# Decay blocks' subtractions issued behind later VectorE work, and the mixer's output product with its first low-input matmuls put last

## Chip, core and metric

The kernel runs on one core of one Trainium2 chip, as one launch. The metric is the device time in microseconds; for the kernel before it is 1547.75 us, the median of three runs (1547.63 to 1549.64).

## What is computed

Two layers (`DEPTH = 2`) of a decoder on a sequence of 256 tokens with 1024 channels, all in fp32. A layer is a half-step SwiGLU FFN, a token mixer, and a second FFN. The mixer normalises its input, multiplies it by one wide matrix and runs two branches on the result: a Mamba-2 branch (SSD, in two chunks of 128 tokens) and a gated DeltaNet branch (four chunks of 64). Both branches' outputs go through a matrix, are gated, added, and multiplied by `w_out`. What matters here, cut from the reference:

```
seg = a_cum[:, :, :, None] - a_cum[:, :, None, :]
decay = jnp.where(causal, jnp.exp(jnp.where(causal, seg, 0.0)), 0.0)
cb = jnp.einsum("bclgn,bcsgn->bclsg", Cc, Bc)
y_diag = jnp.einsum("bclsg,bclsgh,bcsghp->bclghp", cb, decay, xdt)
...
merged = (jax.nn.sigmoid(gate_s) * (y_s @ ssm_w_branch[l])
          + jax.nn.sigmoid(gate_d) * (y_d @ dn_w_branch[l]))
h = h + merged @ w_out[l]
```

The decay is needed for 32 heads; they come in four groups of eight, and a "decay block" is one group's `exp(seg)` for both chunks, masked and multiplied by `cb`: 128 x 2048 numbers.

## The kernel before, in words

**Products.** Every weight tile (128 x 1024) comes in by DMA as `wraw` and is split into two rounded parts: ScalarE (ACT) copies it to `whi` (L67), VectorE (DVE) subtracts to get `wlo` (L70, `prep`, L173 to L194). Inputs are split in the same way into a high and a low part. A product is then three matmuls on TensorE (PE): high x high, high x low, low x high (`mm3`, L315, and `mm3w`, L320). There are five buffers each of `whi` and `wlo` (`NSPL = 5`), taken in turn, so a new `whi` waits until PE has done with the tile five before it.

**The mixer's order.** The mixer is a list of steps written out by hand (`ORDER`, L45 to L49), run by `step` (L1170). Around the change it reads, in the program's order: `P` (`ssd_pre`, L999: for each group the product `cbb` of B and C on PE, masked on DVE into `cbt`), the gate units `g100 g101`, `D0` (`decay(0)`), `S0` (first half of `ssd(0)`, L1048), `x10` (convolved inputs of group 1), `T0` (second half of `ssd(0)`), `D1`, `x11`, gates, `S1`, `x20`, `T1`, `o` (`dn_T(0)`), `x21`, `N` (the DeltaNet branch's matrix, `dn_branch`), `D2`, `y` (`ss_T(0)`), `S2`, `D3` and so on. The scheduler places each engine's instructions in its own queue out of this order; a queue runs in order, and an instruction that waits holds up all that stand behind it.

**decay(g)** (L1020 to L1035): a DMA on SP's queue brings 1 MB of broadcast rows into `dc` (two buffers, `sA` and `sB`, so block 2 takes block 0's); DVE subtracts `ac` (L70, `dc<-dc,ac`); DVE takes the minimum with 0 (L77); ACT takes the exponential (L67, `dc<-dc`); DVE multiplies by `cbt` (L70, `dc<-dc,cbt`). PE reads `dc` in `ssd`'s products `ydb` (L1076).

**ssd(g)**: PE turns the convolved inputs `xsT` (made by ACT behind three DVE steps `ca`) into `xsb` (L1062); DVE scales them to `xD`, `xdt` and `xe`; then `ydb` and `yob` on PE, sums into `yz` on DVE, their squares `jk` on ACT, the sum's `sss` on DVE (L78), a power -0.5 `srr` on GpSimd (POOL, L209), and two scalings of `yz` by it on ACT.

**The DeltaNet branch's matrix**: `dn_T(hp)` (L1111) turns `vb` on PE into `oT` (L1115), DVE gates it to `og`, ACT rounds that to the high part `bh`, DVE subtracts to the low part `bl`. PE multiplies them in `b` (L316 to L318).

**The output product** is `close` (L399), which calls `out_chunks` (L366): for the two row halves t = 0, 1 it takes every weight tile k and column half n. Its input is made by `merge(t)` (L1217): `mT` on PE (L1225), `mh` on ACT, `ml` on DVE. The FFNs' output products go through `close_blocks` and call `out_chunks` without the new argument.

Of the kernel before, what the change touches and what calls it, by code (L numbers as in the profile page):

```python
# [11 lines left out]
ALU = mybir.AluOpType  # L12
# [4 lines left out]
P = 128  # L17
# [7 lines left out]
GS = 4  # L25
# [27 lines left out]
def trunk_kernel(ctx, tc, x, wst, wsm, norms, lpar, rpar, cst, out):  # L53
    nc = tc.nc
    V, A, G, PE = nc.vector, nc.scalar, nc.gpsimd, nc.tensor
# [10 lines left out]
    def act(o, i, func=AF.Copy, **kw):  # L66
        return A.activation(out=o, in_=i, func=func, **kw)  # L67

    def tt(o, a, b, op):
        return V.tensor_tensor(out=o, in0=a, in1=b, op=op)  # L70
# [4 lines left out]
    def ts(o, a, s1, op0, sc2=None, op1=None):  # L75
        if op1 is None:
            return V.tensor_scalar(out=o, in0=a, scalar1=s1, scalar2=None, op0=op0)  # L77
        return V.tensor_scalar(out=o, in0=a, scalar1=s1, scalar2=sc2, op0=op0, op1=op1)  # L78
# [7 lines left out]
    def trb(name):  # L86
        return trp.tile([P, 512], F32, tag="tr", name=name)
# [4 lines left out]
    def small(shape, name, bufs=2):  # L92
        return sm.tile(shape, F32, tag=name, name=name, bufs=bufs)
# [54 lines left out]
    state = {"loaded": 0, "prepped": 0, "taken": 0, "last": None, "hold": False, "behind": {}, "late": {}, "first": 0}  # L148
# [52 lines left out]
    def take():  # L201
        j = state["taken"]
        state["taken"] = j + 1
        ahead("loaded", limit[min(j + NSPL, n_forms) - 1], load)
        ahead("prepped", min(j + 1 if state["hold"] else j + NSPL, n_forms), prep)
        return halves.pop(j)
# [11 lines left out]
    h = cpool.tile([P, 2, D], F32, name="h")  # L218
# [96 lines left out]
    def mm3(ps, lh, ll, rh, rl, start, stop):  # L315
        PE.matmul(ps, lh, rh, start=start, stop=False)  # L316
        PE.matmul(ps, lh, rl, start=False, stop=False)  # L317
        return PE.matmul(ps, ll, rh, start=False, stop=stop)  # L318
# [44 lines left out]
                        cut and a == 0 and kt == 1,  # L363
                    )

    def out_chunks(ps, stat, ks, last, group=1, split=False, first=None):  # L366

        for g0 in range(0, len(ks), group):
            kk = ks[g0 : g0 + group]
            ws = [(k, take()) for k in kk]  # L370
            for t in range(2):
                order = [(k, n) for n in range(2) for k in range(len(kk))]
                if t == 1 and not split:
                    m = len(kk) - 2 if len(kk) == NSPL else len(kk)
                    order = [(k, n) for k in range(m) for n in range(2)]
                    order += [(k, n) for n in range(2) for k in range(m, len(kk))]
                state["sums"] = []
                for k, n in order:
                    k, (wh, wl) = ws[k]
                    sh, sl = stat(k, t)  # L380
                    ins = mm3(
                        ps[t][n][:], sh, sl,
                        wh[:, n * 512 : (n + 1) * 512], wl[:, n * 512 : (n + 1) * 512],
                        k == 0 if first is None else first and t == n == 1, k == last,
                    )
                    state["sums"].append(ins)

    def residual(po, nw):
        def add(t):
            for n in range(2):  # L390
                hv = h[:, t, n * 512 : (n + 1) * 512]
                ins = stt(hv, po[t][n][:], 0.5, hv, ALU.mult, ALU.add)
            return ins

        if nw is None:
            return add
        norm_in(nw, add)

    def close(po, stat, n_k, nw):  # L399

        out_chunks(po, stat, list(range(2)), n_k - 1, group=2)
        out_chunks(po, stat, list(range(2, n_k - NSPL)), n_k - 1)
        state["hold"] = True
        out_chunks(po, stat, list(range(n_k - NSPL, n_k)), n_k - 1, group=NSPL, split=nw is None)
        return residual(po, nw)
# [147 lines left out]
    def mixer(l, nxt):  # L553
# [51 lines left out]
        ac = small([P, 2, 40], "ac", 1)  # L605
# [87 lines left out]
        dE = small([P, 32], "dE", 1)  # L693
# [293 lines left out]
        late = {}  # L987
# [11 lines left out]
        def ssd_pre():  # L999
            BT, CT = late["BC"][:, 0:4], late["BC"][:, 4:8]  # L1000
            cbt = slots.tile([P, 3 * GS, P], F32, tag="sF", name="cbt")
            late["cbx"] = cbx = cbt[:, 2 * GS :]
            late["cbm"] = cbm = cbt[:, : 2 * GS].rearrange("p (g t) l -> p g t l", g=GS)
            for g in range(GS):
                cbb = trb("cbb")
                PE.matmul(cbb[:, 0 : 2 * P], BT[:, g, 0:P], CT[:, g, :], start=True, stop=True)
                PE.matmul(cbb[:, 2 * P : 3 * P], BT[:, g, P : 2 * P], CT[:, g, P : 2 * P], start=True, stop=True)
                tt(
                    cbm[:, g],
                    cbb[:].rearrange("p (t o l) -> p t o l", t=2, o=2)[:, :, 0, :],  # L1010
                    U[:, None, :].to_broadcast([P, 2, P]),
                    ALU.mult,
                )
                act(cbx[:, g], cbb[:, P : 2 * P])
            yield
# [4 lines left out]
        def decay(g):  # L1020
            dc = slots.tile([P, 8, 2, P], F32, tag=("sA", "sB")[g % 2], name="dc")
            nc.sync.dma_start(
                dc[:].rearrange("p h t l -> p (h t l)"),
                rdram[8 * g : 8 * g + 8].rearrange("a b -> (a b)").partition_broadcast(P),
            )
            tt(
                dc[:], dc[:],
                ac[:, :, 8 * g : 8 * g + 8].rearrange("p t h -> p h t")[:, :, :, None].to_broadcast([P, 8, 2, P]),
                ALU.subtract,
            )  # L1030
            dv = dc[:].rearrange("p h t l -> p (h t l)")
            ts(dv, dv, 0.0, ALU.min)
            act(dv, dv, AF.Exp)
            tt(dc[:], dc[:], late["cbm"][:, g, None].to_broadcast([P, 8, 2, P]), ALU.mult)
            decs[g] = dc  # L1035

        def xs_unit(g, i):
# [10 lines left out]
        def ssd(g):  # L1048
            dc = decs[g]
            hs = slice(8 * g, 8 * g + 8)  # L1050

            def bc8(ap):
                return ap[:, :, None].to_broadcast([P, 8, 64])

            def v8(ap):
                return ap.rearrange("p (h d) -> p h d", h=8)

            xd, xt = [], []
            for t in range(2):
                xb_ = trb("xsb")  # L1060
                for k in range(4):
                    PE.transpose(xb_[:, k * P : (k + 1) * P], xsT[g][:, k, t * P : (t + 1) * P], ident)  # L1062
                d1 = tmp2("xD")
                d2 = tmp2("xdt")
                tt(v8(d1[:]), v8(xb_[:]), bc8(dsk[:, hs]), ALU.mult)
                tt(v8(d2[:]), v8(xb_[:]), bc8(sp[:, t, hs]), ALU.mult)
                xd.append(d1)
                xt.append(d2)
            xe = tmp2("xe")
            tt(v8(xe[:]), v8(xt[0][:]), bc8(dE[:, hs]), ALU.mult)  # L1070
            yield
            for t in range(2):
                yb = trb("ydb")
                for hh in range(8):
                    for r in (0, 64):
                        PE.matmul(  # L1076
                            yb[r : r + 64, hh * 64 : (hh + 1) * 64], dc[:, hh, t, r : r + 64],
                            xt[t][:, hh * 64 : (hh + 1) * 64], start=True, stop=True,
                        )
                tt(xd[t][:], xd[t][:], yb[:], ALU.add)  # L1080
            yob = trb("yob")
            PE.matmul(yob[:], late["cbx"][:, g, :], xe[:], start=True, stop=True)
            yo = tmp2("yo")
            tt(v8(yo[:]), v8(yob[:]), bc8(eA[:, hs]), ALU.mult)
            tt(xd[1][:], xd[1][:], yo[:], ALU.add)
            ss = small([P, 2], "sss")
            for t in range(2):
                yv = yz[g][:, t, :]
                tt(yv, yv, xd[t][:], ALU.mult)
                jk = tmp2("jk")  # L1090
                act(jk[:], yv, AF.Square, accum_out=ss[:, t : t + 1])
            ts(ss[:], ss[:], 1.0 / 512.0, ALU.mult, EPS, ALU.add)
            rr = small([P, 2], "srr")
            rsqrt(rr[:], ss[:], [P, 2])
            for t in range(2):
                yv = yz[g][:, t, :]
                act(yv, yv, scale=rr[:, t : t + 1])
            yield
# [115 lines left out]
        ps = branch("s", 8, ss_T)  # L1214
# [20 lines left out]
        po = [[accb("o"), accb("o")] for _ in range(2)]  # L1235
# [12 lines left out]
    for t in range(2):  # L1248
        add(t)
        o = [tmp2("fo") for _ in range(2)]  # L1250
        for n in range(2):
            sl = slice(n * 512, (n + 1) * 512)
# [139 lines left out]
```

## Time and profile before

| | |
|---|---|
| time, median of 3 runs | 1547.75 us (1547.63 to 1549.64) |
| the profiled execution's own time | 1548.12 us |
| its span, first to last instruction | 1546.4 us |
| granted TensorE clock | 0.999 |
| PE busy | 1525.9 us, 99% of the span |
| DVE, ACT, POOL busy | 1228.8, 949.3, 86.9 us |
| the two mixers, from `P` to the end of the output product | about 404 to 598 us and 1168 to 1362 us |

A row of the timeline gives an instruction's start (us from the span's start), its duration, engine, line, what it writes and reads, and, in brackets, how long its engine sat idle before it and what ended that. Matmuls overlap: each starts about 0.23 us (512 columns) or 0.11 us (256 columns) after the one before, though its own row says 0.39 or 0.28 us, so a pause of PE is read from the starts.

### The profile page before, as it was taken

What the parts mean: (1) busy time and instruction counts of PE and PEld (TensorE: products, weight loads), DVE (VectorE), ACT (ScalarE), POOL (GpSimd) and SP (SyncE); (2) the same over time, 40 slices, a digit from 0 to 9 for tenths busy, and PEclk for the clock granted to TensorE, in tenths of its full rate; (3) what the DMA queues carried; (4) which work ended last, traced back from release to release, by engine and by line L of the source; (5) the groups of instructions that cost most, each with busy time, mean ns of one, the idle gap of its engine ahead of it and who ended that gap; (6) DMA issues with size and microseconds to landing.
All of it is one profiled execution on the core that took longest, in us unless ns stands there. A gap on an engine that the chain in (4) does not pass through costs nothing.

```text
span 1546.4 us, 29049 instructions
## 1 busy us (share of the span) xinstructions
PE 1525.9 (99%) x11458; PEld 1383.8 (89%) x11458; DVE 1228.8 (79%) x1856; ACT 949.3 (61%) x1534; POOL 86.9 (6%) x92
## 2 busy tenths in 40 slices
PE   8999999999999999999999999999999999999998
PEld 7999879999888888999899998899998888889996
DVE  6878769967899766788778887789579996678886
ACT  5655667765665645565555566676756665455564
POOL 0000110000000000000100012010000000000010
PEclk9999999999999999999999999999999999999999
DMA  7677765553465455577866687565345555556775
GB/s 273 193 265 228 226 223 169 185 164 110 177 209 172 158 170 192 185 248 214 266 220 226 204 253 236 183 196 184 117 138 203 178 168 184 177 178 190 248 240 156
DMA packets 98831, 305.73 MB, mean 198 GB/s; under 512 B 22837, under 2 KB 23813, under 8 KB 97670
## 3 DMA queue, kind: packets, MB, share of 16 engines
q1 hardware_dynamic: 94086, 291.29, 55.9%
q0 software_dynamic: 4608, 12.58, 4.9%
q8 instruction: 90, 1.47, 0.4%
q14 instruction: 47, 0.39, 0.1%
HBM read 297.72 MB, written 1.92 MB: 194 GB/s over the span
## 4 chain that ended last, share of the span: by engine, by line
PE 86%; DVE 5%; issue 3%; ACT 3%; DMA 2%; POOL 1%; POOLq 0%; SPq 0%; ACTq 0%; DVEq 0%
PE fc L327 9%; PE fc L321 9%; PE fc L326 9%; PE o L318 3%; PE o L317 3%; PE o L316 3%; PE t L316 3%; PE t L317 3%; PE t L318 3%; PE b L318 3%; PE b L316 3%; PE b L317 3%; PE p L317 2%; PE p L316 2%; PE p L318 2%
## 5 line engine op out<-in xcount | busy, mean ns | idle before, releaser
L70 DVE TENSOR_TENSOR wlo<-wraw,whi 128x1024 fp32r<-128x1024 f32 x488 | 592.2, 1221 | 188.1 <-ACT whi L67 174.5
L67 ACT ACTIVATE whi<-wraw 128x1024 fp32r<-128x1024 f32 x488 | 511.6, 1059 | 268.1 <-PE fc L326 91.6
L327 PE MATMUL fc<-uW,wlo 128*128 128x256 f32 x1280 | 354.8, 277 | 0.0
L321 PE MATMUL fc<-uW,whi 128*128 128x256 f32 x1280 | 354.0, 277 | 0.0
L326 PE MATMUL fc<-uW,whi 128*128 128x256 f32 x1260 | 348.2, 276 | 0.0
L321 PEld LDWEIGHTS fc<-uW,whi 128*128 128x128 f32 x1280 | 240.4, 188 | 0.8
L327 PEld LDWEIGHTS fc<-uW,wlo 128*128 128x128 f32 x1280 | 240.6, 188 | 0.0
L326 PEld LDWEIGHTS fc<-uW,whi 128*128 128x128 f32 x1260 | 236.5, 188 | 0.8
L67 ACT ACTIVATE whi<-wsum 128x1024 fp32r<-128x1024 f32 x64 | 68.0, 1062 | 58.8 <-PE fc L326 32.7
L316 PE MATMUL t<-whi,uW 128*128 128x512 f32 x256 | 101.9, 399 | 0.0
L317 PE MATMUL t<-wlo,uW 128*128 128x512 f32 x256 | 100.9, 394 | 0.2 <-DVE wlo L70 0.2
L318 PE MATMUL t<-whi,uW 128*128 128x512 f32 x256 | 100.5, 392 | 0.0
L70 DVE TENSOR_TENSOR wlo<-wsum,whi 128x1024 fp32r<-128x1024 f32 x64 | 78.2, 1222 | 7.9 <-ACT whi L67 5.6
L316 PE MATMUL b<-whi,bh 128*128 128x512 f32 x192 | 76.1, 398 | 0.3 <-ACT bh L67 0.2
L317 PE MATMUL b<-wlo,bh 128*128 128x512 f32 x192 | 74.9, 390 | 0.0
L318 PE MATMUL b<-whi,bl 128*128 128x512 f32 x192 | 74.3, 394 | 0.3 <-DVE bl L70 0.3
L321 PE MATMUL xs<-uW,whi 128*128 128x256 f32 x256 | 72.8, 285 | 0.0
L327 PE MATMUL xs<-uW,wlo 128*128 128x256 f32 x256 | 71.4, 279 | 0.0
L326 PE MATMUL xs<-uW,whi 128*128 128x256 f32 x254 | 70.6, 278 | 0.0
L316 PE MATMUL o<-whi,gh 128*128 128x512 f32 x160 | 62.5, 391 | 0.0
L318 PE MATMUL o<-whi,gl 128*128 128x512 f32 x160 | 62.3, 389 | 0.0
L317 PE MATMUL o<-wlo,gh 128*128 128x512 f32 x160 | 62.3, 389 | 0.0
(332 smaller groups left out, 3401.3 us busy)
## 6 DMA issues: line engine op xcount, KB each, us to landing
wraw<-in_wst_dram SPq DMA_DIRECT2D x504, 512.0 KB, 5.0
wsum<-in_wst_dram SPq DMA_DIRECT2D x16, 512.0 KB, 7.0
wsum<-in_wst_dram POOLq DMA_DIRECT2D x16, 512.0 KB, 8.2
dc<-rdram SPq DMA_DIRECT2D x8, 1024.0 KB, 8.1
nw<-in_norms_dram SPq DMA_DIRECT2D x6, 512.0 KB, 7.5
h<-u POOLq DMA_DIRECT2D x12, 256.0 KB, 6.3
gb<-rdram SPq DMA_DIRECT2D x8, 256.0 KB, 6.0
h<-in_x_dram SPq DMA_DIRECT2D x4, 256.0 KB, 5.6
```

What stands on the lines that cost most here:

```text
L67: return A.activation(out=o, in_=i, func=func, **kw)
L70: return V.tensor_tensor(out=o, in0=a, in1=b, op=op)
L316: PE.matmul(ps, lh, rh, start=start, stop=False)
L317: PE.matmul(ps, lh, rl, start=False, stop=False)
L318: return PE.matmul(ps, ll, rh, start=False, stop=stop)
L321: PE.matmul(ps, wh, mh, start=start, stop=False)
L326: PE.matmul(ps, wh, ml, start=False, stop=False)
L327: PE.matmul(ps, wl, mh, start=False, stop=stop)
```

## The change

`decay` puts each of the first three blocks' subtractions behind an instruction that it names, on the same engine (`tc.issue_after` adds an edge that orders the queue and makes nothing wait on another engine): block 0 behind the four masked products `cbt`, block 1 behind block 0's last product, block 2 behind `xe` of `ssd(1)`; block 3 is left free. `close` asks `out_chunks` to defer, for its first two weight tiles and t = 0, the four matmuls of the low inputs (`ml`) until all eight of the high inputs have been issued. No instruction is added or taken away.

```diff
-    def out_chunks(ps, stat, ks, last, group=1, split=False, first=None):
+    def out_chunks(ps, stat, ks, last, group=1, split=False, first=None, defer=False):
...
-                state["sums"] = []
+                state["sums"], lows = [], []
                 for k, n in order:
                     k, (wh, wl) = ws[k]
                     sh, sl = stat(k, t)
+                    if defer and t == 0:
+                        high, low = (w[:, n * 512 : (n + 1) * 512] for w in (wh, wl))
+                        PE.matmul(ps[t][n][:], sh, high, start=k == 0, stop=False)
+                        PE.matmul(ps[t][n][:], sh, low, start=False, stop=False)
+                        lows.append((ps[t][n], sl, high))
+                        continue
...
+                for bank, sl, high in lows:
+                    PE.matmul(bank[:], sl, high, start=False, stop=False)
...
-        out_chunks(po, stat, list(range(2)), n_k - 1, group=2)
+        out_chunks(po, stat, list(range(2)), n_k - 1, group=2, defer=True)
...
-                tt(
+                late[("cbt", g)] = tt(
                     cbm[:, g],
...
-            tt(
-                dc[:], dc[:],
-                ac[:, :, 8 * g : 8 * g + 8].rearrange("p t h -> p h t")[:, :, :, None].to_broadcast([P, 8, 2, P]),
-                ALU.subtract,
-            )
+            with ExitStack() as behind:
+                for key in ([("cbt", i) for i in range(GS)], [("dec", 0)], [("xe", 1)], [])[g]:
+                    behind.enter_context(tc.issue_after(late[key].ins))
+                tt(
+                    dc[:], dc[:],
+                    ac[:, :, 8 * g : 8 * g + 8].rearrange("p t h -> p h t")[:, :, :, None].to_broadcast([P, 8, 2, P]),
+                    ALU.subtract,
+                )
...
-            tt(dc[:], dc[:], late["cbm"][:, g, None].to_broadcast([P, 8, 2, P]), ALU.mult)
+            late[("dec", g)] = tt(dc[:], dc[:], late["cbm"][:, g, None].to_broadcast([P, 8, 2, P]), ALU.mult)
...
-            tt(v8(xe[:]), v8(xt[0][:]), bc8(dE[:, hs]), ALU.mult)
+            late[("xe", g)] = tt(v8(xe[:]), v8(xt[0][:]), bc8(dE[:, hs]), ALU.mult)
```

The queues of SP and POOL are the same before and after. On DVE, ACT and PE more moves than the diff names, since the scheduler places everything anew around the bound instructions. Both layers move alike; the rows below are the first layer's.

DVE around `P`, before: the first `dc<-dc,ac` is block 0's subtraction; `vb<-ob,os` frees the buffer for which the fourth `cbb` waits.

```order
L70 TENSOR_TENSOR wlo<-wraw,whi 128x1024 x2
L70 TENSOR_TENSOR dc<-dc,ac 128x2048
L70 TENSOR_TENSOR vb<-ob,os 128x512
L70 TENSOR_TENSOR cbt<-cbb,cs 128x256 x2
L965 TENSOR_REDUCE so<-o_4924 128x4
L70 TENSOR_TENSOR cbt<-cbb,cs 128x256
L73 SCALAR_TENSOR_TENSOR so<-so,oe 128x4
L70 TENSOR_TENSOR cbt<-cbb,cs 128x256
L70 TENSOR_TENSOR vb<-vb,so_2310 128x512
L77 TENSOR_SCALAR dc<-dc 128x2048
L70 TENSOR_TENSOR dc<-dc,ac 128x2048
```

The same place after the change:

```order
L70 TENSOR_TENSOR wlo<-wraw,whi 128x1024 x2
L70 TENSOR_TENSOR vb<-ob,os 128x512
L70 TENSOR_TENSOR cbt<-cbb,cs 128x256 x2
L973 TENSOR_REDUCE so<-o_4924 128x4
L70 TENSOR_TENSOR cbt<-cbb,cs 128x256
L73 SCALAR_TENSOR_TENSOR so<-so,oe 128x4
L70 TENSOR_TENSOR cbt<-cbb,cs 128x256
L70 TENSOR_TENSOR vb<-vb,so_2310 128x512
L70 TENSOR_TENSOR dc<-dc,ac 128x2048
L77 TENSOR_SCALAR dc<-dc 128x2048
```

Block 0's subtraction has gone behind the masks, and block 1's (the second `dc<-dc,ac` of the rows before) has left this stretch.

ACT in the same stage, from the conversion that follows `ssd(0)`'s products to the last `xsT` of group 1 and the gate behind it; `dc<-dc` is block 1's exponential, which before the change stood further up, next to block 0's. After the change:

```order
L67 ACTIVATE jk,sss<-yz 128x512
L67 ACTIVATE whi<-wraw 128x1024
L67 ACT_TABLE_LOAD
L67 ACTIVATE dc<-dc 128x2048
L67 ACT_TABLE_LOAD
L67 ACTIVATE xsT<-ca 128x256
L67 ACTIVATE jk,sss<-yz 128x512
L67 ACTIVATE ca<-xs,lp 128x256
L67 ACTIVATE yz<-yz,srr 128x512 x2
L67 ACTIVATE whi<-wraw 128x1024
L67 ACTIVATE xsT<-ca 128x256
L67 ACTIVATE ca<-xs,lp 128x256
```

After these follow three `whi`, a `tg` and the last `xsT`. Before the change both `jk` stood together, with one `whi` and one `ca` between them and the two scalings of `yz`, and no table load among them. The number of table loads in the program is the same, 30.

ACT at the start of `N`, before: `bh<-og` is the high input of the DeltaNet branch's first pair of tiles.

```order
L67 ACTIVATE jk,sss<-yz 128x512
L67 ACTIVATE ca<-xs,lp 128x256
L67 ACTIVATE bh<-og 128x512
L67 ACTIVATE xsT<-ca 128x256
L67 ACTIVATE yz<-yz,srr 128x512 x2
L67 ACTIVATE whi<-wraw 128x1024
```

And after:

```order
L67 ACTIVATE jk,sss<-yz 128x512
L67 ACTIVATE xsT<-ca 128x256
L67 ACTIVATE ca<-xs,lp 128x256
L67 ACTIVATE yz<-yz,srr 128x512 x2
L67 ACTIVATE bh<-og 128x512
L67 ACTIVATE whi<-wraw 128x1024
```

The first `bh` now stands behind the two scalings of `yz`. On PE the twelve transposes `oT` and four transposes `yT` now stand ahead of the first matmul `b`; before, ten `oT` did, and the rest stood among or behind the matmuls.

## The prediction

> **What bounds the kernel now.** I read the page's busy shares first, then PE's waits, then PE's rows around them.
>
> ```profile
> PE 1525.9 (99%) x11458; PEld 1383.8 (89%) x11458; DVE 1228.8 (79%) x1856; ACT 949.3 (61%) x1534; POOL 86.9 (6%) x92
> PE cbb L1006 <- DVE vb L70: 2.9, 2, 1.6
> PE xsb L1062 <- ACT xsT L67: 1.9, 2, 0.9
> PE o L318 <- DVE ml L70: 0.6, 2, 0.3
> PE b L318 <- DVE bl L70: 0.3, 1, 0.3
> ```
>
> PE is busy for 99% of the span, and the change adds no matmul, so it can only close or open pauses of PE. The four waits shown (total, times, longest) are the ones in its reach: 5.7 us together, over both layers. By the starts of the matmuls each costs a little more, since PE's pipeline also runs empty; here is the first layer's `cbb`:
>
> ```profile
> 402.62 1.16 PE L956 MATMUL ob<-vn,AT 128*128 128x128 f32 x8
> 405.50 0.47 PE L318 MATMUL t<-whi,uW 128*128 128x512 f32 x1
> 407.61 0.70 PE L1006 MATMUL cbb<-BC 128*128 128x256 f32 x2 [1.63 <-DVE vb L70]
> ```
>
> From 405.50 to 407.61 there are 2.11 us, of which one matmul of 512 columns takes 0.23: the pause is 1.88 us, 0.25 more than its named 1.63. So the seven pauses behind the four rows are worth at most 5.7 + 7 x 0.25 = 7.5 us, 0.5% of the time.
>
> **The first wait goes.** What PE waits for is a DVE that stands idle for block 0's DMA, and then subtracts before it adds `vb`:
>
> ```profile
> 404.66 2.29 DVE L70 TENSOR_TENSOR dc<-dc,ac 128x2048 f32<-128x2048 f32 x1 [1.81 <-DMA dc<-rdram]
> 406.87 0.68 DVE L70 TENSOR_TENSOR vb<-ob,os 128x512 f32<-128x512 f32 x1
> ```
>
> Behind the masks, the subtraction no longer stands in the way: `ob` ends at 402.62 + 1.16 = 403.8, `vb` follows at once and is done at 404.5, before PE reaches the fourth `cbb` at 405.7. **Term 1: -1.9 us** in the first layer and -1.6 in the second, whose named wait is the other 1.3 of the 2.9. The DMA is issued where it was, since SP's queue is unchanged. The subtraction now waits for the masks and so for PE; behind it on DVE queue its own minimum and the `wlo` of tiles that PE reaches more than 4 us later.
>
> **The `xsT` wait: what is late next.** In the same stage PE waits for the last `xsT` of group 1:
>
> ```profile
> 447.32 0.44 PE L1062 MATMUL xsb<-cs,xsT 128*128 128x128 f32 x2 [0.93 <-ACT xsT L67]
> 442.56 2.28 DVE L70 TENSOR_TENSOR dc<-dc,ac 128x2048 f32<-128x2048 f32 x1
> 446.85 0.42 ACT L67 ACTIVATE xsT<-ca 128x256 f32<-128x256 f32 x1 [1.26 <-DVE ca L73]
> ```
>
> Block 2's subtraction at 442.56 stands among that convolution's steps, and it leaves. But block 1 comes in: its subtraction, minimum, exponential and product now lie between `T0` and this `xsT`, with two table loads. The rows for the new chain:
>
> ```profile
> 411.33 1.07 ACT L67 ACTIVATE whi<-wraw 128x1024 fp32r<-128x1024 f32 x1 [1.34 <-PE t L318]
> 415.54 1.22 DVE L77 TENSOR_SCALAR dc<-dc 128x2048 f32<-128x2048 f32 x1
> 424.14 2.35 DVE L70 TENSOR_TENSOR wlo<-wraw,whi 128x1024 fp32r<-128x1024 f32 x2
> 426.41 0.68 DVE L70 TENSOR_TENSOR xD<-xD,ydb 128x512 f32<-128x512 f32 x1
> 431.18 2.28 DVE L70 TENSOR_TENSOR dc<-dc,cbt 128x2048 f32<-128x2048 f32 x1
> 434.01 1.60 POOL L209 TENSOR_TENSOR srr<-sss,mhalf 128x2 f32<-128x2 f32 x1 [23.59 <-DVE sss L78]
> 435.65 1.34 ACT L67 ACTIVATE yz<-yz,srr 128x512 f32<-128x512 f32 x2 [1.32 <-POOL srr L209]
> 438.15 1.99 ACT L67 ACTIVATE whi<-wraw 128x1024 fp32r<-128x1024 f32 x2
> 441.98 0.58 ACT L67 ACTIVATE tg<-t 128x512 f32<-128x512 f32 x1
> 453.09 1.28 ACT L67 ACT_TABLE_LOAD   x1
> 454.39 1.92 ACT L67 ACTIVATE dc<-dc 128x2048 f32<-128x2048 f32 x1
> ```
>
> DVE first. The two `wlo` of 424.14 move up by 3.0 (`vb` starts at 403.85, not 406.87) and by 1.1 (block 1's minimum has left; its subtraction has left too, but block 0's has come in). They lose about 1.4: DVE waits 0.3 for the last `cbb` and 1.1 for block 0's exponential, which now has two `whi` ahead of it. The second of them gets its buffer 1.4 us (six matmuls) after the first, at 411.3 - 1.9 + 1.4 = 410.8; `whi` 1.0, load 1.3 and exponential 1.9 then end at 415.0. So the `wlo` start at 424.1 - 3.0 - 1.1 + 1.4 = 421.4. Then 2.3 for them, 2.2 for block 1's subtraction, and 4.2 for eight small steps (426.41 to 431.18 are nine, 4.8 us, less one of 0.6): the minimum starts at 430.1 and ends at 431.3.
>
> Now ACT. After the minimum it has one `whi` (1.0), a load (1.3), the exponential (1.9) and a load (1.3): 436.8 at most, and 436.6 if the `whi` starts at 431.1. `xsT` and `jk` end at 437.7, `sss` lets POOL start at 438.0, its 1.60 end at 439.6, two scalings of `yz` take 1.3: 440.9. Then come `whi`, `xsT`, `ca`, three `whi` and `tg`: 1.0 + 0.8 + 2.9 + 0.5, taking each short conversion at the 0.4 to 0.5 between starts. The last `xsT` runs from 446.0 to 446.4, against 446.85 to 447.27. **Term 2: PE leaves this point 1.0 us early** (0.9, and 0.1 for one matmul more that stands ahead of it), not 1.9; 0.7 in the second layer, whose first gain was 0.3 smaller.
>
> [...]
>
> **The start of `N`** is the place that decides.
>
> ```profile
> 460.44 1.25 PE L1115 MATMUL oT<-cs,vb 128*128 128x128 f32 x10
> 461.86 0.50 PE L316 MATMUL b<-whi,bh 128*128 128x512 f32 x1 [0.17 <-ACT bh L67]
> 468.03 0.50 PE L318 MATMUL b<-whi,bl 128*128 128x512 f32 x1 [0.32 <-DVE bl L70]
> 485.22 1.04 PE L1062 MATMUL xsb<-cs,xsT 128*128 128x128 f32 x8
> 1226.38 0.50 PE L316 MATMUL b<-whi,bh 128*128 128x512 f32 x1
> 1249.04 1.04 PE L1062 MATMUL xsb<-cs,xsT 128*128 128x128 f32 x8
> 459.17 1.06 ACT L67 ACTIVATE whi<-wraw 128x1024 fp32r<-128x1024 f32 x1
> 461.19 0.62 ACT L67 ACTIVATE bh<-og 128x512 fp32r<-128x512 f32 x1
> 463.44 1.34 ACT L67 ACTIVATE yz<-yz,srr 128x512 f32<-128x512 f32 x2 [1.32 <-POOL srr L209]
> 461.20 2.21 POOL L209 TENSOR_TENSOR srr<-sss,mhalf 128x2 f32<-128x2 f32 x1 [25.59 <-DVE sss L78]
> 530.39 0.70 POOL L209 TENSOR_TENSOR srr<-sss,mhalf 128x2 f32<-128x2 f32 x1 [18.71 <-DVE sss L78]
> 1225.61 1.61 POOL L209 TENSOR_TENSOR srr<-sss,mhalf 128x2 f32<-128x2 f32 x1 [25.76 <-DVE sss L78]
> ```
>
> Before, `bh` is done at 461.8 and PE starts `b` at 461.86; only then does ACT idle 1.32 us for POOL, and nobody minds. Now `bh` stands behind that wait, and PE, with nothing else in its queue, behind `bh`; so do the next `whi` and DVE's `bl`. The chain cannot slide forward by itself: the `whi` at 459.17 needs a buffer that PE frees some 4 us into `x21`, and `jk`, `sss` and POOL follow it. With PE 1.0 early, POOL starts at 461.2 - 1.0 = 460.2. Its step takes 2.2 in the first layer, the scalings 1.3, `bh` 0.6: PE starts `b` at 464.3. By itself it would be ready at 460.4 - 1.0 + 1.9 = 461.3 (sixteen transposes at 0.12, from the row of ten). **Term 3: a new wait of 3.0 us**, and 2.4 in the second layer with its 1.6. The nearest rows bound POOL's step by 0.70 and 2.21, so the wait by 1.5 and 3.0; I take each layer's own row.
>
> Some comes back: six transposes no longer stand behind the start of `b` (0.7), and the wait at 468.03 (0.5 by the starts) is covered, as `bl` gets more time. From `b` to `xsb` were 23.4 us, now 22.2: `xsb` starts at 486.5 against 485.22, **+1.3 us** for terms 1 to 3. In the second layer `b` starts at 1225.6 - 0.7 + 1.6 + 1.3 + 0.6 = 1228.4; from there 22.7 - 0.7 = 22.0 lead to 1250.4 against 1249.04: **+1.4 us**.
>
> **The output product.**
>
> ```profile
> 574.70 0.39 PE L317 MATMUL o<-wlo,mh 128*128 128x512 f32 x1
> 575.40 0.50 PE L318 MATMUL o<-whi,ml 128*128 128x512 f32 x1 [0.31 <-DVE ml L70]
> ```
>
> `ml` is done by 575.4. With four more matmuls of 0.23 ahead of it the first low one is reached at 575.9, so the pause of 0.47 (0.70 less 0.23) goes. What could be late next is the second half's `mT`, `mh` and `ml`; by PE's queue 19 matmuls stand ahead of the last `mT` where 14 did, so they have more time. **Term 4: -0.5 us per layer.** Nothing else moves on an engine that PE waits for.
>
> **The sum:** 1.3 + 1.4 - 0.5 - 0.5 = **+1.7 us**, from the profiled execution's 1548.12 to 1549.8. That execution lies 0.4 above the runs' median, 1547.75; so I predict **1549.4 us**. The two chains are sums of some ten steps, each known to 0.1 or 0.2, and they come twice: I give the +1.7 an error of 2, so 1547.4 to 1551.4. About 0.2%, 3.1 us, is what a measurement here can tell from no change; the forecast lies within it.
>
> **Rivals.** *The wait for `bh` is hidden, the gains stay* (faster): 1.0 + 0.5 + 0.5 in the first layer, 0.7 + 0.5 in the second, -3.2 us, 1544.5. For it speaks that POOL's step has been as short as 0.70; but with 0.70 in all four chains I still get only -2.5. Against it stand the queue rows: `bh` behind `yz`, in both layers. Chance 0.12.
>
> *DVE becomes the bound in `N`* (slower). Block 2's subtraction and minimum, 3.4 us, move in here:
>
> ```profile
> 462.00:486.00 24.00, 23.68 (x110) 19.13 (x111) 22.20 (x27) 13.12 (x18) 1.41 (x1) 1.00 0.44 139
> ```
>
> DVE, the third busy time, works 22.2 of these 24.0 us; now 25.6, and it idles 2.0 more while it waits for `bh`: 3.6 too much. The first to suffer is the `wlo` of the third pair of tiles, behind three more `bl` and the minimum. I have it done at 477.0, some 12.6 us of queue behind `bh`; PE needs it 58 matmuls after 464.3, at 477.7. From 0.7 us of delay on PE waits, up to 2.9 per layer. Half of that in both gives 1.7 + 2.9 = +4.6, 1552.4 us. Chance 0.25.
>
> [...] Chance 0.05. [...]
>
> **The numbers.** The forecast gets the remaining 0.58. So faster by over 0.2% has 0.12, within 0.2% 0.58, slower by over 0.2% 0.30. The range runs from 1545.0 to 1553.5: it takes in the forecast with its error, POOL's bounds (-2.5 us gives 1545.2) and DVE's rival, and leaves out the table loads and most of the faster rival, about 0.15.
>
> **What would show it.** Right: no wait of PE for `vb`; the `xsb` wait still there, at 1 to 2 us a layer; a wait of `b` for `bh` of over 2 us, right behind a `yz` that POOL released; no wait of `o` for `ml`. Wrong: `b` without that wait, or waits of `b` for `wlo` (DVE's rival), or an idle ACT after its table loads.

## The result and the profile after

The changed kernel takes 1552.57 us, the median of nine runs (1549.35 to 1553.27), against 1547.63 us for the nine runs of the kernel before on the same chip: a ratio of 1.0027, with a 95% interval of 1.0018 to 1.0035. It is slower by 4.9 us, 0.3%. The time lies inside the predicted range, but outside the 0.2% of the likeliest case. The profiled execution took 1553.27 us, 5.15 more than that of before.

The page's first part shows PE busy for as large a share as before:

```profile
PE 1528.9 (99%) x11458; PEld 1387.4 (89%) x11458; DVE 1230.3 (79%) x1856; ACT 948.9 (61%) x1534; POOL 84.5 (5%) x92
```

PE executes the same 11458 instructions and is busy 3.0 us longer. Some of the matmuls themselves must have become longer, not only the pauses between them. PE's waits (total, times, longest) after the change:

```profile
PE b L316 <- ACT bh L67: 4.5, 2, 2.3
PE t L316 <- DVE ca L73: 2.6, 2, 1.3
PE xsb L1073 <- ACT xsT L67: 1.4, 2, 0.7
```

The waits for `vb`, `ml` and `bl` are gone. The wait of `b` for `bh` is there, as predicted. The wait of `t` for `ca` is new, and nothing in the prediction speaks of it.

Where in the mixer the time goes is read between two matmuls that the change doesn't move, the first `cbb` and the first `hnT` of the next FFN. Before, first layer:

```profile
403.62 0.60 PE L1006 MATMUL cbb<-BC 128*128 128x256 f32 x2
...
594.62 1.03 PE L281 MATMUL hnT<-cs,hn 128*128 128x128 f32 x8
```

After:

```profile
404.49 0.60 PE L1014 MATMUL cbb<-BC 128*128 128x256 f32 x2
...
597.81 1.03 PE L281 MATMUL hnT<-cs,hn 128*128 128x128 f32 x8
```

The first mixer grows from 191.00 to 193.32 us, the second (same rows, not shown) from 190.67 to 193.34: together 5.0 of the 5.15 us. The start of `N` divides each mixer: up to the first `b` the two layers lose 1.15 and 1.17 us, behind it 1.17 and 1.50.

**Around `b`.** The rows of POOL, ACT and PE, in order of time:

```profile
460.34 1.60 POOL L209 TENSOR_TENSOR srr<-sss,mhalf 128x2 f32<-128x2 f32 x1 [20.71 <-DVE sss L78]
461.03 0.60 PE L1141 MATMUL yT<-cs,yz 128*128 128x128 f32 x4
461.98 1.33 ACT L67 ACTIVATE yz<-yz,srr 128x512 f32<-128x512 f32 x2 [1.16 <-POOL srr L209]
463.21 0.61 ACT L67 ACTIVATE bh<-og 128x512 fp32r<-128x512 f32 x1
463.88 0.50 PE L316 MATMUL b<-whi,bh 128*128 128x512 f32 x1 [2.25 <-ACT bh L67]
...
465.82 1.05 PE L318 MATMUL b<-whi,bl 128*128 128x512 f32 x2
466.68 0.63 PE L316 MATMUL b<-whi,bh 128*128 128x512 f32 x1
467.10 0.63 PE L317 MATMUL b<-wlo,bh 128*128 128x512 f32 x1
```

The chain is the predicted one: POOL, two scalings, `bh`, and PE with nothing to do; by the starts the pause is 2.41 us. But behind it the matmuls start every 0.43 us instead of 0.23, with 0.63 in their rows instead of 0.39. The windows view shows why. Each of its rows gives a stretch and its length, then the busy time of PE, PEld, DVE, ACT and POOL with the number of their instructions; the granted clock is the third number from the end.

```profile
465.30:468.70 3.40, 3.40 (x10) 2.67 (x9) 3.40 (x7) 1.50 (x3) 0.00 (x0) 0.51 0.46 137
1229.80:1233.20 3.40, 3.37 (x8) 2.72 (x9) 3.38 (x6) 1.56 (x2) 0.00 (x0) 0.52 0.64 218
```

The granted clock falls to half for about 3.4 us, 1.5 us after `b` has started in the first layer and 0.1 us after it in the second. Eight matmuls cost 0.20 more each: 1.6 us per layer.

**Behind `N`.** PE waits for DVE a second time, and the rows of DVE show a late queue:

```profile
469.09 2.28 DVE L70 TENSOR_TENSOR dc<-dc,ac 128x2048 f32<-128x2048 f32 x1
473.33 1.22 DVE L77 TENSOR_SCALAR dc<-dc 128x2048 f32<-128x2048 f32 x1
490.25 2.28 DVE L70 TENSOR_TENSOR dc<-dc,cbt 128x2048 f32<-128x2048 f32 x1
499.64 2.28 DVE L70 TENSOR_TENSOR dc<-dc,cbt 128x2048 f32<-128x2048 f32 x1
501.84 0.47 DVE L73 SCALAR_TENSOR_TENSOR ca<-xs,lp,ca 128x255 f32<-128x255 f32 x1
507.68 2.46 DVE L73 SCALAR_TENSOR_TENSOR ca<-xs,lp,ca 128x255 f32<-128x255 f32 x6
508.20 0.38 PE L1073 MATMUL xsb<-cs,xsT 128*128 128x128 f32 x2
509.89 0.47 PE L316 MATMUL t<-whi,uW 128*128 128x512 f32 x1 [1.31 <-DVE ca L73]
```

Before, the same steps read

```profile
496.02 2.29 DVE L70 TENSOR_TENSOR dc<-dc,cbt 128x2048 f32<-128x2048 f32 x1 [0.77 <-ACT dc L67]
498.23 0.48 DVE L73 SCALAR_TENSOR_TENSOR ca<-xs,lp,ca 128x255 f32<-128x255 f32 x1
...
503.52 2.46 DVE L73 SCALAR_TENSOR_TENSOR ca<-xs,lp,ca 128x255 f32<-128x255 f32 x6
```

Beside block 3's steps, which lay behind the start of `N` before too, block 2's subtraction, minimum and product now all lie there, 5.8 us; before, only its product did, 2.3 us. From the start of `b`, the first `ca` comes after 38.0 us instead of 36.4, and the six together after 43.8 instead of 41.7. `xs`, `t` and `b` take their accumulators (the four tiles of `accp`, which the matmuls write) in turn from one ring (`accb`, L89), so the gate product's `t` can't start before those six have read the convolution: its row names DVE's `ca` behind 1.31 us of idle PE. PE pauses 1.47 us (starts 508.31 to 509.89, less 0.11), and 1.48 in the second layer.

### The profile page after: what moved, and what is told of

It is laid out like the page before. It is cut to its first block, busy times and chain, and to the rows that moved or that the text cites. A ratio compares the mean times of both kernels' runs of the same rounds, so it can differ in the third digit from the quotient of the medians.

```text
span 1551.5 us, 29045 instructions
## 1 busy us (share of the span) xinstructions
PE 1528.9 (99%) x11458; PEld 1387.4 (89%) x11458; DVE 1230.3 (79%) x1856; ACT 948.9 (61%) x1534; POOL 84.5 (5%) x92
## 3 DMA queue, kind: packets, MB, share of 16 engines
q8 instruction: 90, 1.47, 0.4%
## 4 chain that ended last, share of the span: by engine, by line
PE 87%; DVE 6%; ACT 3%; issue 2%; POOL 1%; DMA 0%; SPq 0%; POOLq 0%; ACTq 0%; DVEq 0%
PE fc L327 9%; PE fc L321 9%; PE fc L326 9%; PE t L317 3%; PE o L318 3%; PE o L316 3%; PE o L317 3%; PE t L316 3%; PE b L316 3%; PE t L318 3%; PE b L317 3%; PE b L318 3%; PE p L317 2%; PE p L318 2%; PE p L316 2%
```

## The experiments

All times are medians, of five to eleven runs each; the kernel before ran beside them, and the changed kernel's row has the nine runs of the first result. The pauses are of one profiled execution each, by the matmuls' starts, first layer / second layer; "mixer" is the distance from the first `cbb` to the first `hnT`. Where a wait came in two pieces they are added. A pause at `b` of under 0.4 us is given as 0; the one of e5 is at the second `bh`.

| run | time, us | kernel before | ratio (95%) | mixer | `cbb` | `xsb` | `b` for `bh` | `t` for `ca` | clock at half |
|---|---|---|---|---|---|---|---|---|---|
| before | 1547.63 | | | 191.00 / 190.67 | 1.88 / 1.57 | 1.10 / 1.09 | 0 | 0 | no |
| changed | 1552.57 | 1547.63 | 1.0027 (1.0018 to 1.0035) | 193.32 / 193.34 | 0 | 0.86 / 0.97 | 2.41 / 2.42 | 1.47 / 1.48 | both |
| e1 | 1556.27 | 1547.92 | 1.0057 (1.0045 to 1.0069) | 194.47 / 194.76 | 0 | 0.94 / 0.73 | 3.53 / 3.54 | 0 | both |
| e2 | 1548.72 | 1547.92 | 1.0006 (0.9997 to 1.0014) | 190.41 / 190.41 | 0 | 0.85 / 0.97 | 0 | 1.64 / 1.63 | no |
| e3 | 1547.58 | 1547.92 | 0.9997 (0.9989 to 1.0006) | 190.44 / 190.44 | 0 | 1.57 / 1.72 | 0 | 0 | no |
| e4 | 1552.13 | 1547.92 | 1.0030 (1.0019 to 1.0040) | 192.04 / 191.30 | 1.48 / 0.73 | 0.91 / 1.10 | 2.55 / 2.55 | 0 | no |
| e5 | 1545.80 | 1547.85 | 0.9978 (0.9955 to 1.0001) | 189.44 / 189.45 | 0 | 0.63 / 0.63 | 1.23 / 1.23 | 0 | no |
| e6 | 1550.72 | 1547.85 | 1.0019 (1.0010 to 1.0028) | 191.52 / 191.73 | 0 | 0.97 / 0.97 | 1.60 / 1.54 | 1.51 / 1.48 | no |
| e7 | 1547.20 | 1547.85 | 0.9995 (0.9986 to 1.0003) | 189.76 / 191.61 | 1.41 / 2.33 | 0.88 / 0.30 | 0 | 0 | second, at `cbb` |
| e8 | 1551.93 | 1547.85 | 1.0026 (1.0015 to 1.0036) | 193.35 / 192.95 | 0 | 0.97 / 0.97 | 2.41 / 2.47 | 1.48 / 1.48 | both |
| e9 | 1545.10 | 1547.95 | 0.9983 (0.9974 to 0.9992) | 189.16 / 189.12 | 0 | 0.48 / 0.66 | 0 | 0 | no |
| e10 | 1553.18 | 1547.95 | 1.0032 (1.0020 to 1.0043) | 192.23 / 191.95 | 0 | 0.97 / 0.97 | 2.41 / 2.47 | 1.48 / 1.48 | no |

Beside e5 to e8, one run of the kernel before took 1567.87 us, at a mean granted clock of 0.948; by the medians e5's ratio is 0.9987.

**e1: block 2 free.**

```diff
-for key in ([("cbt", i) for i in range(GS)], [("dec", 0)], [("xe", 1)], [])[g]:
+for key in ([("cbt", i) for i in range(GS)], [("dec", 0)], [], [])[g]:
```

> The changed kernel with block 2's subtraction unbound again (blocks 0 and 1 stay bound, the output product stays deferred). Theory: the gate product's matmul t waits for the convolution steps ca (1.47 us in each layer) because block 2's subtraction, minimum and product now lie in and behind N. Then this wait goes (0 of 1.31 named), while b still waits for bh (over 2 us, since bh still stands behind the two scalings yz). Block 2's subtraction is back among the steps in front of xsT, so the wait of xsb grows from 0.7 named to about 2.5 in the first layer. Time: 2 x 1.5 less and about 2 x 1.7 more than the changed kernel, 1552 to 1554 us. Rival: the late ca comes from all of the blocks' later places, or from PE reaching it earlier, not from block 2; then t still waits over 1 us for ca.

```profile
PE b L316 <- ACT bh L67: 6.7, 2, 3.4
PE yT L1141 <- DVE og L73: 2.2, 2, 1.1
PE xsb L1073 <- ACT xsT L67: 0.9, 3, 0.3
```

The wait of `t` for `ca` is gone in both layers, which is what the run was for: block 2's work in `N` is its cause. That PE only came later isn't the reason: the six `ca` start 39.0 us behind the start of `b`, where the changed kernel had 43.8, and e5 below has the first `b` in time, block 2 free and no such pause, where e2 with block 2 bound has 1.64 us. The rest was misjudged, and the time of 1556.27 us lies above the 1552 to 1554 expected. Block 2's subtraction now comes right behind block 1's product, at 439.1 us and so ahead of the last convolution steps, and `xsb` waits less, not more. In return block 2's exponential and its table loads stand ahead of `jk` on ACT, POOL starts later, and `bh` is 3.5 us late instead of 2.4, with the halved clock behind it.

**e2: the first `bh` ahead.**

```diff
-x11 g110 g111 S1 x20 T1 o x21 N D2 y S2 D3 x30 x31 T2 g000 g010 g001 S3 g011 T3
+x11 g110 g111 S1 x20 o T1 x21 N D2 y S2 D3 x30 x31 T2 g000 g010 g001 S3 g011 T3
```

> The changed kernel with the first dn_T ahead of the second half of ssd(1) in the program's order, so that the first bh stands well ahead of the scalings yz on ACT; the decays stay bound. Theory: b's wait for bh behind POOL's step costs 2.4 us per layer and nothing else hangs on it. Then the wait of b goes, and the time falls by some 3 to 5 us, to 1548 to 1550. The wait of t for ca stays at 1.5 to 3 us per layer, since block 2's work stays where it is and PE arrives earlier. Rival: DVE is the bound from the start of N, and what PE gains at b it loses at the next wait for DVE (wlo, bl or ca); then the time stays within 1 us of the changed kernel's 1552.6.

```profile
PE t L316 <- DVE ca L73: 2.5, 4, 0.9
PE xsb L1073 <- ACT xsT L67: 1.4, 2, 0.7
```

`bh` is done at 456.4 us, and no wait of `b` for it is left. The time falls by 3.9 us, as the theory says, to that of the kernel before. The wait for `ca` stays, in two pieces. So the wait for `bh` and what follows it is not merely exchanged for a wait on DVE.

**e4: the kernel before, with `bh` late.** In `dn_T(0)`:

```diff
+            with ExitStack() as behind:
+                for t in range(2 if hp == 0 else 0):
+                    behind.enter_context(tc.issue_after(late[("yz", 1, t)].ins))
-            act(oh[:].rearrange("p a t -> p (a t)"), og[:])
+                act(oh[:].rearrange("p a t -> p (a t)"), og[:])
```

> The kernel before, with one edit: the first bh is issued on ACT behind the two scalings of yz of ssd(1). Nothing is bound in decay and the output product is as before. It measures the order on ACT by itself. Theory: bh ends at 465.3 instead of 461.8, PE's wait for it is 3.5 us in the first layer and 2.7 in the second, the transposes that move ahead and the covered wait for bl give 1.2 back in each: 1547.6 + 2.3 + 1.5 = 1551.4 us. Rival: the wait is only shown at b and would be had elsewhere (DVE's wlo or ca), so that the time is within 1 us of the kernel before.

```profile
463.62 1.33 ACT L67 ACTIVATE yz<-yz,srr 128x512 f32<-128x512 f32 x2 [0.28 <-POOL srr L209]
464.86 0.61 ACT L67 ACTIVATE bh<-og 128x512 fp32r<-128x512 f32 x1
465.53 0.50 PE L316 MATMUL b<-whi,bh 128*128 128x512 f32 x1 [2.38 <-ACT bh L67]
```

Bound to ACT's order alone, with no decay block bound, the kernel before becomes 4.2 us slower (3.8 expected). One instruction behind two others on ACT is enough for a loss nearly as large as the whole change's. The trace places only a part of it. In the profiled execution, 3.0 us longer than that of before, the clock did not fall, and the mixers lost only 1.0 and 0.6 us; another 1.2 lie ahead of the first mixer, where the kernel is unchanged. The mixers' loss comes with a `cbb` pause that was 0.4 and 0.8 shorter without an edit near it. Three of the eleven runs show a mean granted clock of 0.997 and took 1553.3 to 1557.3 us, the five at 0.999 took 1550.2 to 1552.1.

**e6 and e8: the clock.** e8 is the changed kernel again. e6 differs from it only by eight transposes per layer that fill part of the pause (`yT` written three times with the same values); ACT's and DVE's queues are the same.

```diff
-            for k in range(2):
+            for k in [0, 1] * (3 if j == 0 else 1):
```

> The changed kernel once more, beside the others on one chip. It asks whether the halved clock behind b's wait is in every execution. Theory: the clock's fall depends on when the pause comes, so it can miss; of the runs those with a lower mean granted clock (0.996, two falls) are the longer ones, those with 0.999 (none) are some 3 us shorter. 1549 to 1553.5 us, median 1552.5. Rival: the fall is there in every execution, and the times spread for another reason, without regard to the clock.

> The changed kernel with the four transposes yT ahead of b done three times (the same values written again), eight more of 0.11 us in each layer, all inside PE's pause ahead of b; every other queue keeps its order. bh is as late as before, so b starts at the same time. Theory: behind the pause of 2.4 us the granted clock falls to 0.50 for 3.4 us, so that eight matmuls take 0.43 instead of 0.23, 1.6 us per layer; an idle PE is what causes it. With the pause cut to 1.5 us the clock stays at 1.0 in both layers, and the time falls by up to 3.2 us, to 1549.5 to 1551. Rival: the fall of the clock has nothing to do with the pause; then it shows here too, and the time is that of the changed kernel run beside it.

e6 at `b`, and its granted clock in the two stretches that begin 1.5 us behind `b`'s start:

```profile
460.42 1.47 PE L1141 MATMUL yT<-cs,yz 128*128 128x128 f32 x12
463.33 0.50 PE L316 MATMUL b<-whi,bh 128*128 128x512 f32 x1 [1.43 <-ACT bh L67]
```

```profile
464.80:468.20 3.40, 3.40 (x16) 2.82 (x15) 3.40 (x7) 1.50 (x3) 0.00 (x0) 1.00 0.37 129
1229.30:1232.70 3.40, 3.40 (x16) 2.82 (x15) 3.40 (x7) 1.50 (x3) 0.00 (x0) 1.00 0.34 111
```

The clock stays at 1.0. The mixers are 1.83 and 1.22 us shorter than in e8, and ten of e6's eleven runs have a mean clock of 0.999, where one of e8's eight has. PE executes more and the kernel is 1.2 us faster. That is less than the 3.2 of two falls, and by the mean clocks the two falls aren't in every execution: of the changed kernel's 17 runs (both sets) three have 0.996 and took 1552.7 to 1553.8 us, nine have 0.997 or 0.998 (mean 1552.1), five have 0.999 (mean 1550.8), which is e6's median. The times also spread by some 3 us for reasons that these runs don't show: one run at 0.999 took 1553.0.

**e10 and e7: each part alone.** In e10 `close` calls `out_chunks` without `defer=True`. In e7 nothing is bound:

```diff
-for key in ([("cbt", i) for i in range(GS)], [("dec", 0)], [("xe", 1)], [])[g]:
+for key in ([], [], [], [])[g]:
```

> Only the first part of the change: blocks 0 to 2 bound, the output product's low inputs not deferred. Theory: the two parts add up, the whole loss lies in the first part. Then PE shows the changed kernel's pauses (2.4 us at b, 1.5 us at t behind ca, per layer) and the kernel before's 0.47 to 0.49 at the first low matmul of the output product: 1.0 us more than the changed kernel, 1553.0 to 1553.6 us. Rival: the deferred matmuls cost something elsewhere in the changed kernel; then this one is no slower than it.

> Only the second part of the change: the output product's low inputs deferred, no subtraction bound. Theory: each layer loses the pause of 0.47 to 0.49 at the first low matmul and nothing else changes: 1.0 us less than the kernel before, 1546.6 to 1547, the other pauses of PE as in the kernel before. Rival: the second half's inputs come later or the pause moves to another matmul of the product; then the time is that of the kernel before.

e10's median is 1553.18 us, as expected. Its trace shows the changed kernel's pauses to 0.1 us, and the output product's 0.47 and 0.49. Its profiled execution had no fall of the clock, behind a wait of the same length:

```profile
464.18 0.50 PE L316 MATMUL b<-whi,bh 128*128 128x512 f32 x1 [2.25 <-ACT bh L67]
```

```profile
465.60:469.00 3.40, 3.40 (x17) 2.81 (x16) 3.40 (x7) 1.50 (x3) 0.00 (x0) 1.00 0.41 151
```

In 3.4 us it has 17 matmuls where the changed kernel had 10. From the two traces the fall's price follows a second time: 193.32 - 192.23 + 0.47 = 1.6 us, and 193.34 - 191.95 + 0.49 = 1.9 in the second layer. e7's median is 0.65 us under the kernel before, with 1.0 expected and an interval that includes no difference; in its trace the pause at the first low matmul is gone in both layers and stands nowhere else. By the traces the deferral is worth its 0.5 per layer; the loss is the decay part's.

e7 also had the fall of the clock at another place, behind the longest pause at `cbb`:

```profile
1168.07 0.48 PE L318 MATMUL t<-whi,uW 128*128 128x512 f32 x1
1170.62 1.03 PE L1014 MATMUL cbb<-BC 128*128 128x256 f32 x2 [2.07 <-DVE vb L70]
...
1172.73 0.63 PE L318 MATMUL t<-whi,uW 128*128 128x512 f32 x1
```

**When a pause brings the fall.** The traces' clock records tell. In the changed kernel's trace the clock falls at 465.34, 1229.92 and, as the program ends, 1547.36 us. These are 764.58 and 317.44 us apart: 224 and 93 steps of 3.413 us. The falls of e1, e7 and e8 also lie whole such steps apart. I cut each of the twelve traces, from 25 us on, into these steps, counted back from the fall at its end, and summed PE's busy time in each. A fall follows each of the 20 steps with 1.46 us of PE or less (12 of them at the end of a program), and none of the other 5319, which have 1.56 us or more. So in these traces it matters how much of a pause lies within one step. The step ahead of the first fall in the changed kernel, and the step behind it:

```profile
461.92:465.34 3.42, 1.46 (x6) 1.24 (x7) 2.08 (x4) 2.80 (x4) 0.02 (x1) 1.00 0.79 201
465.34:468.75 3.41, 3.41 (x9) 2.65 (x8) 3.41 (x7) 1.50 (x3) 0.00 (x0) 0.50 0.46 141
```

The same two steps in e10:

```profile
460.34:463.75 3.41, 1.60 (x15) 1.36 (x13) 2.43 (x3) 2.26 (x6) 1.60 (x1) 1.00 0.48 136
463.75:467.17 3.42, 2.99 (x13) 2.49 (x14) 3.01 (x5) 1.96 (x3) 0.00 (x0) 1.00 0.76 253
```

The pause is 2.41 us long in both. In e10 its end lies in the next step, and 1.60 us of PE are left in the first. In e10's second layer and in both layers of e4 the pause is divided between two steps, each with 1.96 us of PE or more. The busy times include the modelled ends of matmuls, so the border holds for this view.

**e3: only the masks.**

```diff
-for key in ([("cbt", i) for i in range(GS)], [("dec", 0)], [("xe", 1)], [])[g]:
+for key in ([("cbt", i) for i in range(GS)], [("cbt", i) for i in range(GS)], [], [])[g]:
```

> Blocks 0 and 1 both bound behind the four masks, block 1 no longer behind block 0's product, block 2 free; the output product stays deferred. Exponentials of blocks 0 and 1 share one pair of table loads again, and bh stands ahead of yz. Theory: the loss of the changed kernel is the order around N, its gains at cbb and at the output product are real. Then no wait of PE for vb, none of b for bh over 0.3, none of t for ca, none of o for ml; the wait of xsb takes back up to 1.5 of the 1.9. Time 1543.5 to 1546, below the kernel before (1547.6). Rival: block 0's subtraction behind the masks itself makes DVE late (the xsT wait takes back all of the 1.9 in both layers, or wlo comes late); then only the output product's 1.0 is left, 1546.5 or more.

```profile
443.29 2.28 DVE L70 TENSOR_TENSOR dc<-dc,ac 128x2048 f32<-128x2048 f32 x1
449.11 0.42 ACT L67 ACTIVATE xsT<-ca 128x256 f32<-128x256 f32 x1 [3.58 <-DVE ca L73]
```

The theory's time was wrong, the rival's right. The waits at `cbb` and for `ca` go and `b` waits only 0.37 us by the starts for `bh`, but the mixers gain only 0.6 and 0.2 us, together less than the output product's 1.0. Block 2's subtraction stands among the convolution steps again, ACT idles 3.58 us for the last `ca`, and `xsb` waits 0.5 and 0.6 longer. That is a part of the 1.9 and 1.6. Most of the rest goes in the rows that follow: `ydb` loses 0.4 us more in each layer, and inside `b` a pause of 0.59 us for `bl` stands in both layers, where before one of 0.48 stood in the first alone. So PE has lost its whole lead by the 24th matmul of `b`. The rival's reason, a late DVE, holds only in part: `xsb` doesn't take back all of the gain.

**e5 and e9: a version that beats both.** e5 is e1's and e2's edit together. e9 adds a second `dn_T` ahead:

```diff
             elif kind == "o":
                 dn_T(0)
+                dn_T(1)
...
-            made = 1
+            made = 2 if kind == "d" else 1
```

> The two edits of the earlier runs together: block 2 unbound (blocks 0 and 1 stay bound), and the first dn_T ahead of the second half of ssd(1); the output product stays deferred. Theory: the changed kernel's loss is two waits and what hangs on them, b for bh behind POOL's step and t for ca behind block 2's work; with both gone its gains are left. From the run with block 2 free (pauses of 11.65 us in the first mixer, of which 3.5 at b, 1.3 at yT and 1.6 of halved clock behind them) some 5.5 to 6.5 us of pauses per mixer remain, against 8.4 and 8.1 before: 4 to 6 us less than the kernel before, 1542 to 1544 us. Rival: the second bh, which now stands behind POOL's step, or wlo is late instead; then a new wait of b of over 1 us shows and the time stays at 1546 or more.

> The run with bh first and block 2 free, with the second dn_T too ahead of the second half of ssd(1), so that the second bh no longer stands behind the scalings yz on ACT. Theory: the pause of 1.23 us that was left at b in each layer is the second bh behind POOL's step, and nothing else is late behind it. Then this pause goes, and the mixers lose up to 2.4 us together: 1543.4 to 1545 us, some 3 to 4 us below the kernel before. Rival: the third bh or DVE's wlo, which have less time, are late in its place; then a pause of about 1 us stands a few matmuls further down and the time stays at 1545.8.

By the medians e5 is 2.05 us faster than the kernel before, not 4 to 6, and its interval just includes no difference. The second `bh` is late in place of the first.

```profile
467.39 0.50 PE L316 MATMUL b<-whi,bh 128*128 128x512 f32 x1 [1.07 <-ACT bh L67]
```

In e9 that wait is gone, and its place is taken by a shorter one for DVE, 13 us behind the first `b`:

```profile
473.84 0.47 PE L316 MATMUL b<-whi,bh 128*128 128x512 f32 x1 [0.58 <-DVE ca L73]
```

Theory and rival both came true in part: 0.7 us of the 2.4 was won. e9 takes 1545.10 us, 2.85 less than the kernel before beside it, 0.9983 (0.9974 to 0.9992), and some 7 less than the changed kernel.

## Why the prediction was partly right and came out too low

- **Term 1, `cbb`: right.** The pauses of 1.88 and 1.57 us are gone; 1.9 and 1.6 were predicted.
- **Term 2, `xsT`: right in kind, too pessimistic.** The last `xsT` was to run from 446.0 to 446.4; it ran from 445.93 to 446.34, but in an execution whose first `cbb` started 0.87 us later. So PE left this point 1.8 and 1.5 us early, not 1.0 and 0.7, and the wait of `xsb` that is left, 0.86 and 0.97 us by the starts, is just under the 1 to 2 that I named. POOL's step took 0.70 there; I had put 1.60. The table loads cost what the rows had said, as the two ahead of this chain show:

```profile
433.10 1.28 ACT L67 ACT_TABLE_LOAD   x1
434.39 1.92 ACT L67 ACTIVATE dc<-dc 128x2048 f32<-128x2048 f32 x1
436.33 1.28 ACT L67 ACT_TABLE_LOAD   x1
437.62 0.42 ACT L67 ACTIVATE xsT<-ca 128x256 f32<-128x256 f32 x1
```

  Each next instruction starts 1.29 us after the load, with nothing between, and so it does behind 25 of this trace's 30 loads; the first stands at the program's start, and behind the other four ACT waits for PE or DVE. The prediction gives a chance of 0.05 to table loads that cost more, and its range leaves them out; no run shows such a cost, and the rows here have the loads' own 1.28 us.
- **Term 3, `bh`: the mechanism was right and its size a little less.** 2.41 and 2.42 us instead of 3.0 and 2.4, since POOL's step in the first layer took 1.60, not 2.21. Because of these two terms `b` starts 1.2 us late where I had 2.4 and 2.0.
- **Term 4, the output product: right**, 0.47 and 0.49, and e7 and e10 show it apart.
- **What failed is the sentence behind the fourth term, "Nothing else moves on an engine that PE waits for", and with it the sum's assumption that a pause costs its own length.** Behind `b` I had the mixers gain 1.6 and 1.1 us; they lose 1.2 and 1.5. Two costs are missing. One is DVE's: `t` waits 1.47 and 1.48 us for `ca`, which e1 removes by freeing block 2, and only that. The other is the clock: a pause of 2.4 us is followed, in both layers of the profiled execution and of e8's, by 3.4 us at half speed, 1.6 us more. Together that is 3.1 us per layer of the profiled execution, 6.2 in both; the overestimate ahead of `b` hides 2.1 of it, and 0.8 of smaller gains behind `b` I have not placed: 1.7 + 6.2 - 2.1 - 0.8 = 5.0.
- **The DVE rival had the right engine and surplus and the wrong place.** It looked for the first sufferer inside `N`, at `wlo`. No `wlo` was late there: the block's product, which nobody needs at once, took the delay, and handed it to the convolution behind `N`, where the ring of accumulators makes PE wait. Its price gave 1552.4 us, and the range held the measured 1552.6 because it took in that price. DVE's wait, 1.5 us per layer, has the size that this rival gave it. That the sum agrees is luck: the clock's 3.2 us, which no rival had, are hidden by 2.9 us of terms that were too pessimistic.

That the idle pause causes the fall is shown by e6, which fills it (1.43 us named are left of 2.25), leaves every other queue's order as it was, and has a clock of 1.0 behind it. The clock's part carries a limit: where a pause lies against the 3.413 us steps differs from execution to execution, and no run here set it, so from the kernel alone a fall is a chance and not a certainty.

## What to carry to other kernels

An instruction that an engine's queue puts behind another one's wait inherits that wait, as `bh` did behind the scalings that waited for POOL (2.41 us of PE): look at each short conversion that TensorE needs at a stage's start, and at what stands ahead of it, before a heavier instruction is moved. When work is pushed into a stage whose engine is full, follow the surplus until it meets a buffer that TensorE reuses; it can come out a stage later, as block 2's did at `t` (1.47 us). And price a pause of TensorE like the one of 2.41 us at `b` with its aftermath, 1.6 us where the clock fell: eight more transposes per layer inside it (e6) made the kernel 1.2 us faster than the changed one beside it.

## What the runs showed of the hardware

- In four of the twelve profiled executions (the changed kernel, e1, e7, e8) the granted clock fell to 0.50 behind a short pause of PE, ahead of the program's end. Pauses of 2.25 to 2.3 us (named) at `b` were followed by it in all four places of the changed kernel's two profiled executions and in neither of e10's two; 3.4 in e1 in both layers; 2.38 us in e4 in neither layer; 2.07 at `cbb` in e7 once; 1.43 in e6 never. It came up to 1.5 us after PE had resumed (changed kernel), or 2.0 us before it (e1, second layer), and lasted 3.41 us, or twice that in e1's second layer, whose long pause (3.54 us by the starts) went on in the step at half rate. In these twelve traces it followed a step of 3.413 us with at most 1.46 us of busy PE, and only such a step; the steps lie differently in each trace.
- The same 128x2 power on POOL took 0.70, 1.60 and 2.21 us in different places and executions (before: at 530.39, 434.01 and 461.20 us; changed, at 460.34: 1.60). For the chain that runs through it here, it is a range, not a number.
- The pause at `cbb` varied between executions without any edit near it: 1.88 and 1.57 before, 1.48 and 0.73 in e4, 1.41 and 2.33 in e7.
